# Convolution branch and gates as a Strassen stage of their own ahead of the attention, in a one-layer streaming encoder on one core

## The chip, the core and the metric

The kernel runs on one core of one Trainium2 chip. Its time is the device time of one execution in microseconds; the profile shows five engines that work side by side: PE (matrix multiply), DVE (vector), ACT (scalar), POOL (GpSimd) and SP, which here only issues DMAs. Before the change the median of three runs is 2145.94 us (2143.27 to 2147.6). Lower is better.

## The reference

One layer, 1024 prompt rows and 32 sample rows (T = 1056 columns in all), model width 1024. In short:

```python
h = rms_norm(x, norm1_g) * (1 + scale1) + shift1       # shift, scale, gate from silu(c) @ w_ada
q, k, v, xin, gb, gc, ga_br, gb_br = split(h @ w_in)   # eight sections of 1024 columns
o = diff_attention(norm(q), norm(k), v)                # 8 heads, chunk-causal for the prompt
y_a = sub_norm(o) @ w_attn_out
y_b = (gb * short_conv(gc * xin)) @ w_conv_out
m = sigmoid(ga_br) * y_a + sigmoid(gb_br) * y_b
x = x + gate1 * (m @ w_out)
x = x + gate2 * ((silu(g) * up) @ w_down)              # g, up = split(norm2(x) @ w_gate_up)
```

## The kernel before, in words

Everything is float32. A matrix operand is split in two parts (`split`: ACT makes the high part, DVE or POOL subtracts it for the low part), and each product is three matmuls: high by high, high by low, low by high. The activations lie transposed, 128 channels by 1056 columns, in eight tiles; a weight piece is 1024 rows by 128 columns.

The program has these stages, in order of time.

- **Head.** Loads x, computes norm1 and the modulation (matmuls of `w_ada`), and writes the split operand `hh`, `hl` (`modulate`). The first attention matmul ends it.
- **Attention and convolution, interleaved.** Per head, eight prompt tiles of 128 rows and one sample tile. A tile is a projection (`proj`, L485 to L487, 24 matmuls of 384 columns) and then five steps in `attend`: transposes of q and k (L372), scores (L397, L398), transposes of the probabilities (L434), probabilities by values (L448), transpose of the result (L461). Between two steps, ACT, DVE and POOL work on the tile: the epilogue, the split of q and k (L359 to L365), the softmax (L403 to L422), the copy of the transposed probabilities (L443), the last norm (L450 to L457). The convolution branch (`conv`, L526 to L528) is 72 units of 24 matmuls of 352 columns, for the sections xin, gc and gb. Its weight pieces are split with POOL for the low part.
- **Gates.** The sections ga and gb, 48 units of 24 matmuls of 352 columns (L687 to L689), each piece followed by one `ada_step`: one of 32 later modulation chunks, 16 DVE instructions (`adacc`) and, one step later, two transposes on PE (`pad`).
- **Attention output projection, convolution output projection, w_out, gate and up, down.** The gate-and-up stage already uses Strassen's product (`strassen`, L1013): of a pair of weight pieces and four quarters of the columns it makes seven products of 12 matmuls of 264 columns in place of eight.

The order of PE's instructions is the order in which the program is written. In the attention stage a small planner in the kernel writes it: it holds a clock that counts an assumed cost of each PE step and an assumed wait behind it (8.0 us behind a projection, 4.0 behind the q and k transposes, 4.5 + 6.5 L/1024 behind the scores, 1.2 and 4.0 behind the next two). A tile's next step is placed as soon as its assumed wait is over, otherwise a projection or a convolution unit is placed. At most MAXRUN = 4 tiles are under way, and behind a head's last projection no new one starts for RELOAD = 9.0 us, because the next head's weights take the place of the old. The order on the other engines is set by the compiler's scheduler.

PSUM in the attention stage has two buffers `mm` for projections, two `tr` for all transposes and small products (steps 1, 3, 4 and 5, one after the other in rotation; step 3 takes two when it has over four blocks), and two `S` for scores. The head's weights `qh`, `ql` have one buffer, and are staged in two: the third of the three sections is loaded when the first has been split.

```python
MAXRUN, RESERVE, RELOAD = 4, 3, 9.0
...
if pnext is not None and len(running) < MAXRUN and clock >= hold and (
        cnext is None or pdone * (9 * KT - RESERVE) <= cdone * 9 * H):
    unit_now, kind = pnext, 0
elif cnext is not None and (pnext is not None or True):
    unit_now, kind = cnext, 1
```

Of the kernel before, what the change touches and what calls it, by code (L numbers as in the profile page):

```python
# [14 lines left out]
P = 128  # L15
# [23 lines left out]
def hybrid_layer(tc, x_prompt, x_sample, cache_k, cache_v, state_conv, c_prompt, c_sample,  # L39
# [19 lines left out]
    m1_d = dram.tile([KT, P, T], F32, name="m1_d")  # L59
# [6 lines left out]
    hTp = sb("hT", side="right")  # L66
# [18 lines left out]
    def wload(src, hi, lo, lo_eng=None, v=None):  # L85
        if v is None:
            v = stage()[:, :1024].rearrange("p (a b) -> p a b", a=src.shape[1])
        sp.dma_start(v, src)
        split(v, hi, lo, lo_eng)

    def wpiece(src, lo_eng=None):
        hi = W.tile([P, KT, P], F32R, tag="wh", name="wh", bufs=2)
        lo = W.tile([P, KT, P], F32R, tag="wl", name="wl", bufs=2)
        wload(src, hi, lo, lo_eng)
        return hi, lo
# [23 lines left out]
    hh = hTp.tile([P, KT, T], F32R, name="hh")  # L119
    hl = hTp.tile([P, KT, T], F32R, name="hl")  # L120
    hS = hTp.tile([P, KT, P], F32R, name="hS")
    dve.memset(f(hS), 0.0)

    qW = sb("qW")

    def load_qkv(h):
        hi = qW.tile([P, 3, KT, P], F32R, tag="qh", name="qh")
        lo = qW.tile([P, 3, KT, P], F32R, tag="ql", name="ql")
        for j in range(3):
            v = qW.tile([P, KT, P], F32, tag="qst", name="qst", bufs=2)  # L130
            wload(win_v[:, :, j * D + h * P:j * D + (h + 1) * P], hi[:, j], lo[:, j], None, v)
        return hi, lo


    X0 = sb("X0")
    PS0 = ps("PS0")
    vec = const.tile([P, P], F32, name="vec")
    sc = const.tile([P, 16], F32, name="sc")
    pv = PS0.tile([P, 512], F32, tag="b", name="pv", bufs=2)
# [9 lines left out]
    def rows_to_vec():  # L149
        pv = PS0.tile([P, 512], F32, tag="b", name="pv", bufs=2)  # L150
        pe.transpose(pv[:, :P], rows, ident)
        dve.tensor_copy(vec, pv[:, :P])
# [6 lines left out]
    def attention_constants():  # L159
        lams = X0.tile([P, 4, HD], F32, name="lams")  # L160
# [6 lines left out]
        lprod = X0.tile([P, 2, HD], F32, name="lprod")  # L167
        dve.tensor_mul(lprod, lams[:, 0:2, :], lams[:, 2:4, :])
        lsum = X0.tile([P, 2], F32, name="lsum")
# [14 lines left out]
    xts = {}  # L184

    def x_norm(i):

        src, n = token_tile(i)
        xt = X0.tile([P, D], F32, tag="xt", name="xt", bufs=5)
        sp.dma_start(xt[:n], src)  # L190
        junk = X0.tile([P, D], F32, tag="junk", name="junk", bufs=1)
# [4 lines left out]
        xts[i] = xt, n  # L196

    def x_transpose(tiles, kts):
        q0 = tiles[0] * P
        w = sum(xts[i][1] for i in tiles)  # L200
        for kt in kts:
            pt = PS0.tile([P, 512], F32, tag="x", name="pt", bufs=4)
# [1025 lines left out]
```

## Time and profile before

| what | value |
|---|---|
| median of the runs | 2145.94 us (2143.27 to 2147.6) |
| the profiled execution's own time | 2149.89 us |
| its span, first to last instruction | 2148.1 us |
| PE, DVE, ACT, POOL busy, share of the span | 96%, 57%, 36%, 18% |
| granted PE clock, mean | 0.987 |
| head | 0 to 64.1 us |
| attention and convolution | 64.1 to 906.6 us |
| gates | 906.6 to 1097.0 us |
| both output projections | 1097.0 to 1287 us |
| w_out, gate and up, down | 1287 to 2148 us |

A row of the grouped view gives line, engine, operation, output and input tiles, shapes and count, then the busy time and the mean of one in ns. Matmuls overlap, so the mean of one (about 325 ns for 352 columns) is longer than the step from one to the next; the step is read from a stage's length and its count. A row of the view by windows gives a stretch, its length, the busy time and instruction count of PE, PE's weight loads, DVE, ACT and POOL, then the granted PE clock, the DMA share and GB/s.

### The profile page before, as it was taken

What the parts mean: (1) busy time and instruction counts of PE and PEld (TensorE: products, weight loads), DVE (VectorE), ACT (ScalarE), POOL (GpSimd) and SP (SyncE); (2) the same over time, 40 slices, a digit from 0 to 9 for tenths busy, and PEclk for the clock granted to TensorE, in tenths of its full rate; (3) what the DMA queues carried; (4) which work ended last, traced back from release to release, by engine and by line L of the source; (5) the groups of instructions that cost most, each with busy time, mean ns of one, the idle gap of its engine ahead of it and who ended that gap; (6) DMA issues with size and microseconds to landing.
All of it is one profiled execution on the core that took longest, in us unless ns stands there. A gap on an engine that the chain in (4) does not pass through costs nothing. (4 is left out here: it accounts for less than half of the span.)

```text
span 2148.1 us, 36100 instructions
## 1 busy us (share of the span) xinstructions
PE 2060.6 (96%) x13955; PEld 2014.5 (94%) x13955; DVE 1215.7 (57%) x2775; ACT 770.8 (36%) x1875; POOL 384.8 (18%) x644
## 2 busy tenths in 40 slices
PE   7899999999999999999999999879999999989999
PEld 5799998989899989899999999879999999989998
DVE  5665656575747465556567884576555556432322
ACT  5344445454545444423221112363332332321210
POOL 2333323333333332200000000002112112100000
PEclk9999999999999999999999999999999999999999
DMA  9312122121212110255567634223222222551321
GB/s 261 86 45 60 43 61 60 46 58 46 71 34 72 34 50 23 58 162 180 170 210 224 205 113 142 66 70 108 83 80 84 76 80 74 174 156 53 109 69 57
DMA packets 286195, 206.93 MB, mean 96 GB/s; under 512 B 12976, under 2 KB 269768, under 8 KB 286024
## 3 DMA queue, kind: packets, MB, share of 16 engines
q1 hardware_dynamic: 286024, 204.63, 31.5%
q8 instruction: 110, 1.80, 0.4%
q14 instruction: 61, 0.50, 0.1%
HBM read 153.74 MB, written 50.84 MB: 95 GB/s over the span
## 5 line engine op out<-in xcount | busy, mean ns | idle before, releaser
L82 ACT CAST ws<-st 128x512 fp32r<-128x512 f32 (+1 forms) x280 | 170.1, 614 | 451.4 <-PE u L1013 107.1
L83 DVE TENSOR_TENSOR ws<-st,ws 128x512 fp32r<-128x512 f32 (+1 forms) x258 | 179.4, 701 | 248.6 <-ACT ws L82 246.8
L1013 PE MATMUL u<-T,ws 128*128 128x264 f32 x1848 | 237.6, 285 | 7.8 <-ACT T L82 6.5
L1013 PEld LDWEIGHTS u<-T,ws 128*128 128x128 f32 x1848 | 230.2, 189 | 8.4 <-ACT T L82 6.7
L526 PE MATMUL mm<-hh,wh 128*128 128x352 f32 x576 | 199.2, 346 | 0.0
L528 PE MATMUL mm<-hh,wl 128*128 128x352 f32 x576 | 188.6, 327 | 0.0
L527 PE MATMUL mm<-hl,wh 128*128 128x352 f32 x576 | 188.3, 327 | 0.0
L485 PE MATMUL mm<-qh,hh 128*128 128x384 f32 x512 | 184.3, 360 | 3.0 <-ACT hh L82 2.9
L487 PE MATMUL mm<-qh,hl 128*128 128x384 f32 x512 | 174.5, 341 | 0.0
L486 PE MATMUL mm<-ql,hh 128*128 128x384 f32 x512 | 173.9, 340 | 0.0
L1013 PE MATMUL u<-B,ws 128*128 128x264 f32 x1320 | 170.9, 283 | 0.0
L1013 PEld LDWEIGHTS u<-B,ws 128*128 128x128 f32 x1320 | 164.2, 188 | 0.2 <-ACT p L1017 0.2
L1130 PE MATMUL u<-ka,ws 128*128 128x352 f32 x480 | 157.6, 328 | 4.6 <-ACT ka L82 2.9
L1131 PE MATMUL u<-ka,ws 128*128 128x352 f32 x480 | 156.5, 326 | 2.6 <-DVE ka L83 2.6
L1132 PE MATMUL u<-ka,ws 128*128 128x352 f32 x480 | 156.1, 325 | 0.0
L414 ACT ACTIVATE p<-S,nmx,rs 128x128 f32<-128x128 f32 (+5 forms) x144 | 113.5, 790 | 117.5 <-DVE nmx L410 76.5
L242 DVE SCALAR_TENSOR_TENSOR adacc<-adw,sc,adacc 128x128 f32<-128x128 f32 x448 | 130.6, 349 | 0.6
L687 PE MATMUL u<-hh,ws 128*128 128x352 f32 x384 | 125.9, 328 | 0.0
L689 PE MATMUL u<-hh,ws 128*128 128x352 f32 x384 | 124.9, 325 | 0.0
L688 PE MATMUL u<-hl,ws 128*128 128x352 f32 x384 | 124.2, 323 | 0.0
L687 PE MATMUL u<-oh,ws 128*128 128x352 f32 (+1 forms) x384 | 123.2, 321 | 0.0
L689 PE MATMUL u<-oh,ws 128*128 128x352 f32 (+1 forms) x384 | 121.0, 315 | 0.0
(263 smaller groups left out, 4767.5 us busy)
## 6 DMA issues: line engine op xcount, KB each, us to landing
st<-in_w_gate_up_dram SPq DMA_DIRECT2D x44, 512.0 KB, 4.1
adw<-in_w_ada_dram SPq DMA_DIRECT2D x43, 512.0 KB, 4.3
st<-in_w_in_dram SPq DMA_DIRECT2D x40, 512.0 KB, 4.3
qst<-in_w_in_dram SPq DMA_DIRECT2D x24, 512.0 KB, 4.7
sa<-a_d SPq DMA_DIRECT2D x22, 528.0 KB, 3.7
a_d<-xa SPq DMA_DIRECT2D x84, 132.0 KB, 1.8
st<-in_w_down_dram SPq DMA_DIRECT2D x16, 512.0 KB, 4.3
z_d<-z SPq DMA_DIRECT2D x24, 176.0 KB, 2.7
```

Of the source, the lines that this page charges most:

```text
L82: act.copy(hi, src)
L83: (lo_eng or dve).tensor_sub(lo, src, f(hi))
L485: pe.matmul(pj[:, 0:384], a, qh[:, :, kt, :], start=kt == 0, stop=False)
L486: pe.matmul(pj[:, 0:384], a, ql[:, :, kt, :], start=False, stop=False)
L487: pe.matmul(pj[:, 0:384], b, qh[:, :, kt, :], start=False, stop=kt == KT - 1)
L526: pe.matmul(pt[:, :gw], wh[:, kt, :], hh[:, kt, g0:g0 + gw], start=kt == 0, stop=False)
L527: pe.matmul(pt[:, :gw], wh[:, kt, :], hl[:, kt, g0:g0 + gw], start=False, stop=False)
L528: pe.matmul(pt[:, :gw], wl[:, kt, :], hh[:, kt, g0:g0 + gw], start=False, stop=kt == KT - 1)
L687: pe.matmul(pt[:, :gw], wh, ah[:, kt, g0:g0 + gw], start=kt == 0, stop=False)
L689: pe.matmul(pt[:, :gw], wl, ah[:, kt, g0:g0 + gw], start=False, stop=kt == KT - 1)
L1013: pe.matmul(q[dst], l, t[:, r, j, :], start=first and j == n == 0, stop=j == 3 and n == 2, skip_group_check=not first)
L1130: pe.matmul(pt[:, :gw], wh, ah, start=kt == 0, stop=False)
```

## The change

Five of the eight sections (xin, gc, gb, ga, gb_br) are computed by `strassen` in a dense stage ahead of the attention. `h_operands` makes the seven operands of the activations for each of the two column groups right behind the modulation, and the modulated x is also written to memory (`h_d`). The convolution is done on pairs of channel tiles, between the Strassen products of gc and gb. The two gate sections follow, with two `ada_step` for each pair. Then `h_d` is loaded back, tile by tile, and split as the operand of q, k and v (`hA`), in the slots of the Strassen operands.

The attention follows without the convolution units. The planner has MAXRUN = 5 and RELOAD = 7.0, and when a head's weights hold it up it places nothing. When no projection is left, units of the convolution's output projection (`wco_units`) fill its last part; the rest of them and the attention's output projection follow, with the operand tiles in other slots. In the head, x is loaded first and the `w_ada` chunks behind it; the modulation matmul has weights and activations exchanged (`ada_matmul`).

The diff, cut to its core:

```diff
-    hh = hTp.tile([P, KT, T], F32R, name="hh")
-    hl = hTp.tile([P, KT, T], F32R, name="hl")
...
+    def h_operands(j, g):
+        def parts(o, src):
+            t = Top[o, g]
+            split(src, t[:, 0, j, :], t[:, 1, j, :])
+        b11, b12 = (xnT[:, j, q * QW:(q + 1) * QW] for q in (g, g + 2))
+        b21, b22 = (xnT[:, j + 4, q * QW:(q + 1) * QW] for q in (g, g + 2))
+        t1, t2, t3 = (X0.tile([P, QW], F32, tag=f"t{i}", name="ht", bufs=1) for i in (1, 2, 1))
+        parts("B11", b11)
+        dve.tensor_sub(t1, b12, b11)
+        dve.tensor_sub(t2, b22, t1)
+        parts("T2", t2)
+        parts("T1", t1)
...
+    for j in range(4):
+        for i in range(4):
+            ada_matmul()
...
+        modulate(j)
+        modulate(j + 4)
+        h_operands(j, 0)
+        if j:
+            h_operands(j - 1, 1)
+    for n in range(KT):
+        sp.dma_start(h_d[n], xnT[:, n, :])
+    h_operands(3, 1)
...
+    for p in range(0, KT, 2):
+        xin = pair_tile()
...
+            conv_in(wstrassen(win_pair(3, p)), p, (0, 1), xin)
+        w = wstrassen(win_pair(5, p))
...
+        conv_gate(w, p, u, xin)
+        w = wstrassen(win_pair(4, p))
...
+        conv_out(w, p, z)
...
+    for sec, dst in ((6, ga_d), (7, gb_d)):
+        for p in range(0, KT, 2):
+            w = wstrassen(win_pair(sec, p))
...
+            strassen(w, (0, 1), dest, epi)
+            ada_step()
+            ada_step()
+    while ada_open:
+        ada_open.pop(0)()
...
+    for t in range(8):
+        v = kt_stage(hv[:, :, t * P:(t + 1) * P])
+        hA.append(op_slot(t, [P, 2, KT, P], F32R, "hA"))
+        split(v, hA[t][:, 0], hA[t][:, 1])
...
-    MAXRUN, RESERVE, RELOAD = 4, 3, 9.0
+    MAXRUN, RELOAD = 5, 7.0
...
-            if pnext is not None and len(running) < MAXRUN and clock >= hold and (
-                    cnext is None or pdone * (9 * KT - RESERVE) <= cdone * 9 * H):
-                unit_now, kind = pnext, 0
-            elif cnext is not None and (pnext is not None or True):
+            if pnext is not None:
+                if len(running) < MAXRUN and clock >= hold:
+                    unit_now, kind = pnext, 0
+            elif running and cnext is not None:
                 unit_now, kind = cnext, 1
...
-    for sec, dst in ((6, ga_d), (7, gb_d)):
-        for n in range(KT):
-            w = wpiece(win_v[:, :, (sec * KT + n) * P:(sec * KT + n + 1) * P])
...
-                unit(pt, w, hh, hl, g0, gw)
-                act.activation(sg[:, g0:g0 + gw], pt[:, :gw], AF.Sigmoid)
-            sp.dma_start(dst[n], sg)
...
-            ada_step()
```

Two places show how the order moves. The first is PE at the end of a middle head, from the sample tile's last projection matmuls (`hS`) on. Before, convolution matmuls (L526 to L528) follow, with steps of the tiles under way among them:

```order
2576 L511 MATMUL mm<-qh,hS 128x384
2577 L512 MATMUL mm<-ql,hS 128x384
2578 L526 MATMUL mm<-hh,wh 128x352
2579 L527 MATMUL mm<-hl,wh 128x352
2580 L528 MATMUL mm<-hh,wl 128x352
2581 L526 MATMUL mm<-hh,wh 128x352
2582 L527 MATMUL mm<-hl,wh 128x352
2583 L528 MATMUL mm<-hh,wl 128x352
2584 L461 MATMUL tr<-ident,on 128x128
```

After, the last result transpose (L697), the q and k transposes of the eighth tile (L608), the probability transposes of the sixth (L670, six of them), its values product (L684) and the scores of the eighth (L633, L634) stand one behind the other, and the next head's projection (L721) is next:

```order
1492 L748 MATMUL mm<-ql,hS 128x384
1493 L697 MATMUL tr<-ident,on 128x128
1494 L608 MATMUL tr<-ident,qd 128x128 x2
1495 L608 MATMUL tr<-ident,kd 128x128 x2
1496 L670 MATMUL tr<-ident,p 128x128 x6
1497 L684 MATMUL tr<-V,aT 128x128 x6
1498 L633 MATMUL S<-K,QH 128x512
1499 L634 MATMUL S<-K,QL 128x512
...
1505 L634 MATMUL S<-K,QL 128x512
1506 L721 MATMUL mm<-qh,hA 128x384
```

What moved: the convolution matmuls that stood between the steps are gone, and steps that use the two `tr` buffers follow each other directly.

The second is DVE in the gates stage. Before, each weight piece (two `ws`) has one `adacc` group of 16:

```order
1252 L251 TENSOR_REDUCE adred<-pad 128x2
1253 L239 TENSOR_SCALAR adacc<-adw,sc 128x128
1254 L252 TENSOR_SCALAR mod<-adred,vec 128x2
1255 L242 SCALAR_TENSOR_TENSOR adacc<-adw,sc,adacc 128x128
1256 L239 TENSOR_SCALAR adacc<-adw,sc 128x128
1257 L242 SCALAR_TENSOR_TENSOR adacc<-adw,sc,adacc 128x128 x12
1258 L83 TENSOR_TENSOR ws<-st,ws 128x512
1259 L242 SCALAR_TENSOR_TENSOR adacc<-adw,sc,adacc 128x128
1260 L83 TENSOR_TENSOR ol<-st,oh 128x1056
1261 L83 TENSOR_TENSOR ws<-st,ws 128x512
```

After, for each pair of pieces, two such groups stand among the weight sums and splits (L142 to L152, L84) and the sums of the Strassen products (L183, L186, L192):

```order
660 L183 TENSOR_TENSOR u_5481<-u,p_5451 128x264
661 L332 SCALAR_TENSOR_TENSOR adacc<-adw,sc,adacc 128x128 x5
662 L186 TENSOR_TENSOR w<-u,u_5466 128x264
663 L332 SCALAR_TENSOR_TENSOR adacc<-adw,sc,adacc 128x128 x4
664 L186 TENSOR_TENSOR w<-u,u_5481 128x264
665 L332 SCALAR_TENSOR_TENSOR adacc<-adw,sc,adacc 128x128 x4
666 L84 TENSOR_TENSOR ws<-st,ws 128x512
667 L332 SCALAR_TENSOR_TENSOR adacc<-adw,sc,adacc 128x128
668 L142 TENSOR_TENSOR st<-st 128x512
669 L84 TENSOR_TENSOR ws<-st,ws 128x512
670 L144 TENSOR_TENSOR st<-st 128x512
671 L147 TENSOR_TENSOR st<-st 128x512
```

What moved: the modulation chunks stand in a stage whose products also need DVE for every sum, and on PE the last chunk's two transposes stand ahead of the first attention matmul.

629 lines of the change are left out of this document (325 added, 304 removed).

## The prediction

> **What bounds the kernel now.** I read the page's busy times first, then the view by windows, cut at the stages, then PE's waits and the rows behind them.
>
> ```profile
> PE 2060.6 (96%) x13955; PEld 2014.5 (94%) x13955; DVE 1215.7 (57%) x2775; ACT 770.8 (36%) x1875; POOL 384.8 (18%) x644
> ```
>
> ```profile
> 0.00:64.10 64.10, 43.86 (x347) 31.73 (x347) 39.75 (x97) 33.40 (x73) 20.41 (x31) 1.00 0.92 257
> 64.10:906.60 842.50, 807.78 (x5096) 780.51 (x5096) 504.63 (x1194) 395.56 (x1179) 277.38 (x522) 0.98 0.17 50
> 906.60:1097.00 190.40, 190.40 (x1185) 189.81 (x1184) 106.78 (x334) 50.85 (x93) 0.00 (x0) 0.99 0.56 169
> 1429.60:1867.00 437.40, 437.37 (x3596) 437.37 (x3597) 250.09 (x460) 142.07 (x284) 79.92 (x86) 1.00 0.29 86
> ```
>
> PE is the bound: it is never idle in the gates (third row) and in gate-and-up (fourth), and in the attention stage it is busy 807.8 of 842.5 us. Those 35 us are mostly one kind of wait:
>
> ```profile
> PE tr L461 <- DVE on L457: 21.0, 13, 2.2
> L457 DVE SCALAR_TENSOR_TENSOR on<-o,rn,gsub x72: 339/352/2440, 99.9 to 906.0; 128x128 f32<-128x128 f32 x64, 32x128 f32<-32x128 f32 x8
> L83 POOL TENSOR_TENSOR wl<-st,wh 128x1024 fp32r<-128x1024 f32 x24 | 58.1, 2420 | 34.1 <-ACT wh L82 34.0
> ```
>
> The last norm of a tile on DVE takes 0.35 us, but up to 2.44 where one of the 24 convolution weight splits on POOL (2.42 us) runs, and PE then waits about 2 us. What such a wait does to PE's speed shows in the time line behind one of them:
>
> ```profile
> 766.99 0.30 PE L461 MATMUL tr<-ident,on 128*128 128x128 f32 x1 [2.03 <-DVE on L457]
> ...
> 768.30 0.50 PE L526 MATMUL mm<-hh,wh 128*128 128x352 f32 x1
> 768.60 0.50 PE L527 MATMUL mm<-hl,wh 128*128 128x352 f32 x1
> ...
> 771.65 0.32 PE L526 MATMUL mm<-hh,wh 128*128 128x352 f32 x1
> 771.80 0.32 PE L527 MATMUL mm<-hl,wh 128*128 128x352 f32 x1
> ```
>
> Matmuls of 352 columns start 0.30 us apart for some 3.4 us after the wait, and 0.16 apart later: PE runs at half its clock for that time and loses about 1.7 us more.
>
> **The matmuls that go.** The chain of waits has gate-and-up as one piece:
>
> ```profile
> 1429.63 433.59 PE u L1013 x3563
> ```
>
> So a Strassen matmul of 264 columns costs 433.59 / 3563 = 0.1217 us. One of 352 columns costs 190.40 / 1184 = 0.161 us (the gates row). The change turns 5 sections x 8 pieces x 3 groups x 24 = 2880 matmuls of 352 into 5 x 4 pairs x 7 x 2 x 12 = 3360 of 264: 463.7 becomes 408.9 us. That is the gain, 55 us: in the convolution 278.2 (1728 x 0.161) becomes 245.3 (2016 x 0.1217), in the gates 185.5 becomes 163.6. All the rest is about what the convolution had been covering.
>
> **Gates: DVE takes the bound.** Durations from the Strassen stage and from the gates of before:
>
> ```profile
> L83 DVE TENSOR_TENSOR ws<-st,ws 128x512 fp32r<-128x512 f32 x126 | 91.6, 728 | 91.9 <-ACT ws L82 90.4
> L988 DVE TENSOR_TENSOR st<-st 128x512 f32<-128x512 f32 x21 | 15.0, 712 | 0.7
> L1020 DVE TENSOR_TENSOR u<-u,p 128x264 f32<-128x264 f32 x42 | 17.9, 427 | 4.7 <-PE u L1013 4.7
> L242 DVE SCALAR_TENSOR_TENSOR adacc<-adw,sc,adacc 128x128 f32<-128x128 f32 x224 | 63.7, 349 | 0.1
> L239 DVE TENSOR_SCALAR adacc<-adw,sc 128x128 f32<-128x128 f32 x32 | 8.8, 282 | 0.6 <-PE u L689 0.6
> L251 DVE TENSOR_REDUCE adred<-pad 128x2 f32<-128x256 f32 x14 | 5.9, 425 | 11.1 <-PE pad L249 11.1
> ```
>
> A gate pair asks DVE for 6 low parts, 4 weight sums and 10 product sums: 6 x 0.73 + 4 x 0.71 + 10 x 0.43 = 11.5 us. Two modulation chunks add 2 x (14 x 0.349 + 2 x 0.282 + 0.425 + some 0.3) = 12.4. So DVE needs 23.9 us for a pair whose matmuls take 168 x 0.1217 + 0.4 = 20.9. Only two chunks can run ahead (two `adacc` buffers), so 7 of 8 pairs are paced by DVE: 20.9 + 7 x 23.9 = 188. The last chunk starts only when its buffer is free, behind the last pair, and its transposes stand ahead of the first attention matmul, so its 5.5 us of DVE lie in the open; the first pair, which has no chunk beside it, gives part of that back. I take 190, no gain against 190.4. Bounds are 167 (all of DVE hidden, 8 x 20.9) and 197 (the last chunk and some of the split of `hA`, which is DVE work too, on top).
>
> **Head and convolution.** The head of before moved 257 GB/s (first row of the windows). x now comes first, 4.3 MB or 17 us; norm, transposes and four chunks of `w_ada` bring the first operands to about 35. Their rows:
>
> ```profile
> 25.59 3.82 PE L205 MATMUL pt<-ident,xt 128*128 128x128 f32 x32
> 29.34 1.91 PE L221 MATMUL pa<-adw,sc 128*2 128x128 f32 x16
> ```
>
> From there DVE sets the pace: in its order 61 instructions of 264 columns, 10 of 512 and some 24 small ones stand ahead of the low part that the first product waits for. At 0.38 (0.728 scaled to 264 columns; 0.43 with PSUM) that is 23 + 7 + 5.5 = 36 us. First matmul near 72 (bounds 64 and 78), 8 later than before. The convolution then needs 245 us of PE. A pair of its channel tiles takes 3 x 20.4 = 61 us of PE and, on DVE, 3 x 11.5 and some 12 for the taps, which PE's matmuls hide; were they not hidden, each pair would cost what DVE is over 61. I add 5 us for a start at half clock and for second-group operands that are made late: 250 (247 to 260). The stores of `h_d` and its loads (4.3 MB each way) run on DMA queues that were 0.17 to 0.56 busy in these stages; on SP the stores stand ahead of the loads for the second product, which has 20 us until it needs them. I count them at nothing.
>
> [...]
>
> **Attention without filler.** The stage of before, less 278 for the convolution, is 564.5 us: 530 of PE busy and 35 of waiting. What waits now is read from measured latencies along the new order. Three rules give nearly all of it. First, the weights:
>
> ```profile
> L512 PE MATMUL mm<-ql,hS x3: 334/334/334, 576.2 to 576.9; 128*128 128x384 f32 x3
> L82 ACT CAST qh<-qst x3: 1046/1047/1052, 577.1 to 583.9; 128x1024 fp32r<-128x1024 f32 x3
> L83 DVE TENSOR_TENSOR ql<-qst,qh x3: 1217/1224/1226, 578.2 to 585.0; 128x1024 fp32r<-128x1024 f32 x3
> L485 PE MATMUL mm<-qh,hh x1: 338/338/338, 589.7 to 589.7; 128*128 128x384 f32 x1
> ```
>
> The last sample matmul ends at 577.3, the third low part at 586.2: a reload takes 9.0 us, and before, the next projection came at 12.4, behind convolution work. RELOAD is now 7.0, and the order has only some 4.5 us of matmuls there. Second, the two `tr` buffers:
>
> ```profile
> 508.45 0.38 PE L372 MATMUL tr<-ident,kd 128*128 128x128 f32 x2
> ...
> 509.23 0.47 ACT L359 ACTIVATE K<-tr,gq 128x256 fp32r<-128x256 f32 x1
> ...
> 509.59 0.37 ACT L361 CAST QH<-tr 128x256 fp32r<-128x256 f32 x1
> ...
> 510.78 0.42 DVE L365 TENSOR_TENSOR QL<-tr,QH 128x256 fp32r<-128x256 f32 x1
> ```
>
> The q and k transposes end at 508.83 and their buffer is read until 511.20: 2.4 us, of which the instructions themselves are 0.47 + 0.37 + 0.42 = 1.3. A step that needs the same buffer two uses later now follows at once, where convolution matmuls stood between. Third, the copy behind the probability transposes:
>
> ```profile
> L443 DVE COPY aT<-tr 128x512 f32<-128x512 f32 x8 | 5.4, 675 | 0.6 <-PE tr L434 0.6
> ```
>
> ```profile
> 772.12 0.40 PE L397 MATMUL S<-K,QH 128*128 128x512 f32 x1
> 772.36 0.40 PE L398 MATMUL S<-K,QL 128*128 128x512 f32 x1
> ```
>
> The copy takes about 0.9 us with its start, and the values product can now follow the transposes directly. The two score rows give the step of a score matmul, 0.24 us.
>
> At the end of a head (second piece of the order) this gives: L697 and the eighth tile's transposes take 0.5 us, four of the six L670 0.4, the fifth waits 2.4 - 0.4 = 2.0 for the buffer, it and the sixth take 0.2, L684 waits 0.9 and takes 1.3, the scores take 8 x 0.24 = 1.9, and L721 finds 7.2 of the 9.0 us gone and waits 1.8. The waits are 4.7 us for a head.
>
> Inside a head the same rule meets, by the order, the fourth tile's transposes (1.3), the fifth's (2.0), the sample cache's (0.9) and one or two later ones (0.3 to 2): another 5 to 6. So about 10 us a head, 80 in all; 8 at the shortest latencies of the trace, 13 to 17 if the denser stage slows the chains (DVE was 60% busy, and the same work without the convolution's now falls in three quarters of the time). With four waits of about 2 us a head, of which roughly every other one of before was followed by the half clock at 1.7 us, the clock costs 25, where in the 530 of before it cost about 17 (a granted clock of 0.98 over 842.5). With 5 of those 8 on top I take 85: 530 + 85 = 615. Bounds: 565, for idle of 35 as before, and 670, for 17 a head.
>
> [...]
>
> **The sum.** 72 + 250 + 190 + 615 = 1127 up to the point where before stood at 1097.0; the output projections and all that follows keep their matmuls (four units of the convolution's projection, 15 us, move up into the attention's last part; I count them where they were). 2148.1 + 30 = 2178; the profiled execution lies 1.8 above its span and 4 above the median. On the median: 2145.9 + 30 = **2176 us**.
>
> **The rivals.** *A: the attention fills itself.* With POOL's long splits gone the chains come down to their own instructions, 1.3 to 1.8 us for the buffer, so idle is 45 to 60 in place of 85; and the scheduler hides part of the modulation chunks, gates 178. Then 70 + 248 + 178 + 585 = 1081: 16 us faster, 2130; at best, with every bound at its low end, 2100. For it speaks that nearly half of the 2.4 us was waiting in a queue; against it that the reload and the buffer rotation are fixed by buffer counts. It decides when the attention's idle time stays below 55 us, with the other terms as taken. *B: the half clock settles in.* If each of some 40 waits of 2 us or more costs a window of 3.4 us, and the in-order queues of DVE and ACT add a microsecond to each chain, each head waits 17 us, 140 in all, and the attention takes 670: 72 + 250 + 190 + 670 = 1182, 85 slower, 2231. Against it: only about half of such waits did so before. *C: it cancels.* Idle of 51 to 59 us with the other terms as taken makes the sum 1093 to 1101, within 4 us of before: 2146.
>
> **How the numbers follow.** Forecast (slower by 10 to 65 us) 0.50, A 0.27, B 0.15, C 0.08. A difference under 0.2%, 4 us, cannot be told from none here. The range reaches into A and B until a tenth is left out on each side: 2118 to 2224; the forecast's own is 2156 to 2211. Faster 0.27, same 0.08, slower 0.65.
>
> **What would show it.** In the changed profile: PE busy in 0.12 us steps through the convolution with hardly a gap; a gates stage near 190 us with DVE close to full; in the attention PE waits at L721 for `ql` at each head (1 to 4 us), at L670 and L684 for the q and k split or the copy, and more stretches at half clock. I am wrong if the gates are near 167, or if PE's idle time in the attention is under 55 us.

## The result, and the profile after

The changed kernel takes 2253.74 us (2249.89 to 2259.23, four runs) against 2146.55 us (2143.27 to 2147.6, four runs): a ratio of 1.0504, 95% interval 1.0476 to 1.0532. It is 107 us slower, 78 us above the forecast and 30 above the range. The page of the changed kernel has these two lines for the engines' busy time and the clock in 40 slices:

```profile
PE 2081.6 (92%) x14419; PEld 2018.5 (89%) x14419; DVE 1377.8 (61%) x3128; ACT 841.6 (37%) x2033; POOL 392.9 (17%) x688
```

```profile
PEclk7699999998999999999899999999999999999999
```

PE's busy time did not fall, though 55 us of matmuls went; it rose by 21, and the span rose by 109. The view by windows, cut at the stages (head, convolution, gates, attention, the attention's last part with four units of the convolution's projection), has the columns of the prediction (length, then busy time and count of PE, weight loads, DVE, ACT and POOL, then granted clock, DMA share and GB/s):

```profile
0.00:82.90 82.90, 66.77 (x330) 64.54 (x331) 40.17 (x113) 39.66 (x80) 9.58 (x24) 0.67 0.64 208
82.90:342.40 259.50, 250.27 (x2017) 249.34 (x2018) 202.20 (x408) 73.07 (x142) 67.81 (x98) 0.97 0.26 77
342.40:519.20 176.80, 167.36 (x1379) 166.56 (x1376) 155.12 (x423) 66.89 (x140) 13.07 (x11) 0.98 0.50 154
519.20:1184.60 665.40, 558.84 (x3267) 508.51 (x3268) 400.31 (x999) 356.94 (x1097) 207.37 (x450) 0.93 0.17 50
1184.60:1215.90 31.30, 29.96 (x199) 27.34 (x198) 20.00 (x47) 15.97 (x46) 6.49 (x15) 1.00 0.27 83
```

| stage | before | predicted | measured |
|---|---|---|---|
| head | 64.1 | 72 | 82.9 |
| convolution | 278.2 | 250 | 259.5 |
| gates | 190.4 | 190 | 176.8 |
| attention without filler | 564.5 | 615 | 681.2 |
| sum | 1097 | 1127 | 1200 |

The attention's figure is 665.4 + 31.3, less 15.5 for the 96 filler matmuls in it. The two Strassen stages together brought 32 us (18.7 and 13.6), where the forecast had 28, all of it in the convolution. The head lost 18.8 and the attention 117; what follows takes 6 us more. PE's waits by what it waited for (us in total, times, longest):

```profile
PE tr L670 <- ACT ot L699: 18.5, 15, 4.3
PE tr L670 <- ACT aT L679: 12.7, 8, 3.8
PE tr L697 <- DVE QL L601: 12.1, 9, 2.1
...
PE mm L721 <- ACT qh L83: 7.2, 3, 2.5
PE S L634 <- DVE QL L601: 6.7, 7, 2.3
PE tr L697 <- DVE on L693: 6.7, 5, 1.7
```

Where before one kind of wait made most of the idle time, now no single one has a fifth of the 108 us. The longest one, in the time line of PE and ACT:

```profile
840.46 0.27 PE L697 MATMUL tr<-ident,on 128*128 128x128 f32 x1
...
840.48 1.04 ACT L83 CAST qh<-st 128x1024 fp32r<-128x1024 f32 x1 [2.08 <-PE mm L747]
...
841.43 1.09 ACT L650 ACTIVATE p<-S,nmx,rs 128x896 f32<-128x896 f32 x1
...
842.51 1.03 ACT L83 CAST qh<-st 128x1024 fp32r<-128x1024 f32 x1
...
844.07 1.10 ACT L650 ACTIVATE p<-S,nmx,rs 128x896 f32<-128x896 f32 x1
...
845.15 0.26 ACT L699 COPY ot<-tr 128x128 f32<-128x128 f32 x1
...
845.46 0.90 PE L670 MATMUL tr<-ident,p 128*128 128x128 f32 x3 [4.30 <-ACT ot L699]
```

The result of a tile is transposed by 840.73, and its copy takes ACT 0.26 us. But the copy stands in ACT's queue behind two weight casts, two exponentials and a short copy, which ACT works off with hardly a gap (3.36 us busy of the 3.41 from 840.92 on), and PE needs that `tr` buffer back: 4.30 us.

What such a wait does to the clock shows in windows of 3.41 us, cut where the granted clock changes (the clock is the column behind POOL's):

```profile
837.50:840.92 3.42, 3.42 (x22) 3.20 (x20) 1.53 (x3) 1.22 (x4) 1.06 (x3) 1.00 0.00 0
840.92:844.33 3.41, 0.24 (x3) 0.01 (x1) 3.21 (x7) 3.36 (x6) 0.00 (x0) 1.00 0.00 0
844.33:847.74 3.41, 1.30 (x5) 0.90 (x6) 3.28 (x7) 3.41 (x11) 0.30 (x2) 0.50 0.80 216
847.74:851.16 3.42, 2.15 (x9) 1.75 (x9) 2.56 (x6) 0.71 (x1) 1.79 (x4) 0.50 0.42 122
851.16:854.57 3.41, 3.41 (x13) 2.93 (x12) 0.33 (x3) 0.77 (x3) 0.76 (x2) 0.50 0.54 154
854.57:857.99 3.42, 3.42 (x21) 2.77 (x19) 3.00 (x7) 1.92 (x5) 0.00 (x0) 1.00 0.00 0
```

A window in which PE works 0.24 us is followed by one at half clock; that one has 1.30 us of work, and the next is at half clock too, and so on, until a window full of work (the fifth row) ends it: in the last row the clock is full.

### The profile page after: what moved, and what is told of

Its sections match the earlier page's. It is cut to its first block, busy times and chain, and to the rows that moved or that the text cites. A ratio compares the mean times of both kernels' runs of the same rounds, so it can differ in the third digit from the quotient of the medians.

```text
span 2257.4 us, 37877 instructions
## 1 busy us (share of the span) xinstructions
PE 2081.6 (92%) x14419; PEld 2018.5 (89%) x14419; DVE 1377.8 (61%) x3128; ACT 841.6 (37%) x2033; POOL 392.9 (17%) x688
## 5 line engine op out<-in xcount | busy, mean ns | idle before, releaser
L83 ACT CAST ws<-st 128x512 fp32r<-128x512 f32 (+1 forms) x388 | 234.9, 615 | 576.3 <-PE u L176 177.9
L176 PE MATMUL u<-op,ws 128*128 128x264 f32 x3168 | 393.5, 284 | 7.8 <-ACT op L83 6.5
L176 PEld LDWEIGHTS u<-op,ws 128*128 128x128 f32 x3168 | 388.7, 189 | 8.4 <-ACT op L83 6.7
L84 DVE TENSOR_TENSOR ws<-st,ws 128x512 fp32r<-128x512 f32 (+1 forms) x346 | 242.3, 707 | 201.5 <-ACT ws L83 199.0
L721 PE MATMUL mm<-qh,hA 128*128 128x384 f32 x512 | 188.6, 368 | 8.4 <-ACT qh L83 7.2
L722 PE MATMUL mm<-ql,hA 128*128 128x384 f32 x512 | 175.6, 343 | 2.1 <-DVE ql L84 2.1
L723 PE MATMUL mm<-qh,hA 128*128 128x384 f32 x512 | 175.3, 342 | 0.0
L84 POOL TENSOR_TENSOR ws<-st,ws 128x512 fp32r<-128x512 f32 x42 | 55.1, 1311 | 491.7 <-ACT ws L83 434.3
L721 PEld LDWEIGHTS mm<-qh,hA 128*128 128x128 f32 x512 | 99.0, 193 | 12.0 <-ACT qh L83 8.1
L580 POOL TENSOR_TENSOR rs<-rs,mhalf 128x2 f32<-128x2 f32 x144 | 101.1, 719 | 5.9
L722 PEld LDWEIGHTS mm<-ql,hA 128*128 128x128 f32 x512 | 98.9, 193 | 3.4 <-DVE ql L84 3.1
L1202 PEld LDWEIGHTS u<-ka,ws 128*128 128x128 f32 x480 | 91.6, 191 | 8.4 <-ACT ka L83 5.6
L684 PE MATMUL tr<-V,aT 128*128 128x128 f32 (+2 forms) x608 | 92.3, 301 | 7.1 <-DVE QL L601 3.1
```

The lines of the kernel that those rows point to most:

```text
L83: act.copy(hi, src)
L84: (lo_eng or dve).tensor_sub(lo, src, f(hi))
L176: pe.matmul(q[dst], l, t[:, r, j, :], start=first and j == n == 0, stop=j == 3 and n == 2, skip_group_check=not first)
L580: pool.tensor_tensor(out=rs[:n, c:c + 2], in0=rs[:n, c:c + 2], in1=mhalf[:n, 0:2], op=ALU.pow)
L721: pe.matmul(pj[:, 0:384], a, qh[:, :, kt, :], start=kt == 0, stop=False)
L722: pe.matmul(pj[:, 0:384], a, ql[:, :, kt, :], start=False, stop=False)
```

## The experiments

Theory after the result: without filler, PE meets the latency of each step's answer, and it pays for that in idle time and in half clock. The rivals: one buffer ring is short (`tr`; a ring is a set of buffers used in rotation), one queue is too full (ACT's or DVE's), the planner's distances are too short, the weight reload blocks the end of each head, or the new stages and layout themselves are slower. Totals are medians of two runs, to be held against 2254 us (its own runs differ by 9 us, so differences under some 5 us say nothing). "Net" is the attention's length less 0.161 us for each filler matmul in it, 681 us in the changed kernel and 564 before.

**Filler back in.** Dummy units stand where the convolution's units stood, placed by the rule of before.

```diff
-    MAXRUN, RELOAD = 5, 7.0
+    def fill_units():
+        for i in range(72):
+            def run(i=i):
+                pt = mm_tile()
+                x = hA[(i + 1) % 8][:, 0].rearrange("p k c -> p (k c)")[:, :GW]
+                for kt in range(KT):
+                    for n in range(3):
+                        pe.matmul(pt[:, :GW], hA[i % 8][:, n % 2, kt, :], x, start=kt == n == 0,
+                                  stop=kt == KT - 1 and n == 2)
+                    yield 3 * 0.161
+            yield run()
...
+    MAXRUN, RESERVE, RELOAD = 4, 3, 9.0
...
```

> 72 units of 24 matmuls of 352 columns on the resident operand, whose sums nobody reads, stand in the attention where the kernel before had its convolution, by that kernel's rule of order (MAXRUN 4, RELOAD 9.0); the convolution's projection units all follow behind the attention. The units are 278 us of matmuls at 0.161 us. If the lost filler is the cause, the attention takes 278 + 530 + 35 to 45 of idle time = 843 to 855 us, so 565 to 577 without the units, and the total is 2395 to 2420. If the dense stage, the new layout or the crowded engines were the cause, the attention takes 278 + 640 to 681 and the total is 2490 to 2530.

Measured: 2387.79 us, below what was expected. The attention takes 822.0 us:

```profile
516.50:1338.50 822.00, 804.39 (x5096) 772.82 (x5096) 423.93 (x1037) 378.59 (x1137) 217.77 (x464) 0.99 0.14 40
```

PE is idle 17.6 us, and the net is 544: 137 less than in the changed kernel and 20 less than before. So the layout, the operands and the engines' load are not what costs; the missing independent matmuls are. The planner's old rule does not explain it either: with that rule and no filler a head takes 96.5 us (below). Much of the 20 us below the kernel before is the wait for the last norm on DVE, 21.0 us there and 4.9 here. With POOL's 24 convolution splits gone that norm takes 0.35 us at most in the changed kernel (up to 2.44 before).

**The buffer ring.** The values product and the result's transpose use `mm`.

```diff
-        po = tr_tile()
+        po = mm_tile()
...
-        pt = tr_tile()
+        pt = mm_tile()
         pe.transpose(pt[:, :n], on[:n], ident[:n, :n])
```

> The values product and the transposes of a tile's result take their PSUM buffer from the ring mm, which only the projections use otherwise, so the ring tr serves the q and k transposes and the probability transposes alone. Ring theory (a step waits because the buffer two uses back is still being read; the two waits of L670 and L697 are 66 of the 109 us that PE idles in the attention): at least 40 us of that idle time go, and some 15 us of half clock with it; total 2195 to 2215. Queue theory (the answers of ACT and DVE are late whatever buffer is used): the waits move to the projections and to L684, the idle time stays above 95 us; total 2240 to 2260.

Measured: 2253.7 us, idle 110.4 us. The waits moved:

```profile
PE tr L670 <- ACT aT L679: 27.9, 12, 6.0
PE mm L721 <- ACT sq L575: 13.5, 10, 2.4
```

The ring theory, which was also the frame of my forecast, fell. At L670 the waits on `ot` are gone, and others, as long, came up there and at the projections. The run moves load from one pair of buffers to another and adds none, so whether there are too few buffers in all is not tested.

**One queue for another.**

```diff
-        act.copy(ot[:, :n], pt[:, :n])
+        dve.tensor_copy(ot[:, :n], pt[:, :n])
```

> The copy of a tile's result out of PSUM (L699, 0.28 us) is made by DVE in place of ACT. If the buffer is held long because ACT's queue has long exponentials in front of that copy, the 15 waits of L670 on it (18.5 us) go and the total falls to 2225 to 2240. If DVE's queue, 60% busy in this stage, is as late, as many waits stand there with DVE as the releaser and the total stays within 8 us of 2254.

Measured: 2270.71 us, 17 more than the changed kernel, which neither side expected; idle 124.2 us. Waits for `ot` fell from 18.5 to 7.9 us at L670, and a wait that was hardly there (0.5 us) took their place, behind DVE's longer queue:

```profile
PE tr L670 <- DVE QL L601: 22.9, 6, 6.2
```

**The reverse.** The second copy of the probabilities goes from DVE to ACT.

```diff
-                (act.copy if b0 == 0 else dve.tensor_copy)(aT[:w, i0:i1, :n], pt[:w, i0:i1, :n])
+                act.copy(aT[:w, i0:i1, :n], pt[:w, i0:i1, :n])
```

> The copy of the fifth to eighth transposed probability block (L679, 32 times in the attention, 0.4 to 0.7 us) is made by ACT in place of DVE, the reverse of the move of 20 us from ACT to DVE that cost 17 us. If DVE is the queue that counts, 8 to 17 us less, 2237 to 2246. If every queue counts alike, or the two copies side by side were worth more, the total stays the same or rises: 2250 to 2270.

Measured: 2240.47 us, 13 less, as if DVE were the queue that counts; but in the traces the attention accounts for 7 us (689.8 in place of 696.8), and the head, which this edit does not touch, for 3.4.

**Less in DVE's queue.**

```diff
-        dve.scalar_tensor_tensor(out=kd[HD:P], in0=ksrc[HD:P], scalar=gq[HD:P], in1=f(kd[HD:P]),
-                                 op0=ALU.mult, op1=ALU.subtract)
```

> Left out: the subtraction that makes the low part of the keys on partitions 64 to 127 (L598, 0.49 us on DVE, 63 times in the attention, 31 us), so that the keys are the high part alone. It stands ahead of the query's low part in DVE's queue. If the waits are made by the load of the in-order queues, the idle time falls by 20 us or more and the total by 20 to 40 us, to 2214 to 2234. If they are made by distances in the order or by buffers, it falls by what the one chain is shorter where PE waits for QL (22 us in 19 waits of about 1.2 us): under 12 us, total 2242 to 2250.

Measured: 2236.42 us, 17 less, with idle time of 94.5 us, 13 less: between the two cases. So I took the larger load of the row maximum out as well:

```diff
-                dve.tensor_reduce(out=nmx[:n, m:m + 1], in_=sv[m][:n], axis=AX.X, op=ALU.max, negate=True)
-                dve.tensor_mul(nmx[:n, m:m + 1], nmx[:n, m:m + 1], rs[:n, m:m + 1])
...
-            act.activation(p[:n, :L], sv[m][:n], AF.Exp, bias=nmx[:n, m:m + 1], ...
+            act.activation(p[:n, :L], sv[m][:n], AF.Exp, bias=zero1[:n], ...
```

> Left out: the row maximum of the scores and its product with the norm (L639, L640, L645, L646, some 105 us of DVE in the attention); the exponentials take a bias of zero, and the scores are a quarter of what they should be so that they stay finite. Queue theory (what is in DVE's queue sets when a tile's answers come; 31 us less of DVE gave 16 us, 20 us moved onto DVE cost 17): 50 to 85 us less, total 2170 to 2205, idle time of PE in the attention below 70 us. If only the length of one chain or the order counts, the two score buffers are read some 1.4 us less and a tile's answer comes as much earlier, but PE still waits at L670 and L697 for ACT's copies: 10 to 30 us less, total 2225 to 2245.

Measured: 2245.24 us (2241.71 and 2248.77), just beyond the second case. DVE has 322 us of work in the attention where the changed kernel had 420 (400.31 + 20.00), the time from the last score matmul to the blended probabilities is 3.5 us in place of 5.6 (medians), and PE is still idle 101.7 us. The largest wait grew, from 18.5 us:

```profile
PE tr L668 <- ACT ot L697: 27.9, 19, 3.7
```

So the load of DVE's queue is not the cause either; a hundred microseconds less of it gave some 8. Whether the same work counts where there is filler:

> The kernel before, with the same left out as in the changed kernel without row maximum (and the scores a quarter). If convolution work hides what DVE does in the attention, the total changes by less than 6 us, 2140 to 2150. If DVE's time counts there too, it falls as far as in the changed kernel, 50 us or more.

Measured: 2152.89 us for the kernel before with the same left out, 1.0025 (1.0013 to 1.0036) of its time, though DVE has 390 us of work in the attention in place of 505. With filler the maximum was hidden altogether.

**More distance.** MAXRUN 7, longer assumed waits, one to three more buffers for twelve small tiles.

```diff
-    MAXRUN, RELOAD = 5, 7.0
+    MAXRUN, RELOAD = 7, 7.0
...
-        yield 0.43, 4.0
+        yield 0.43, 6.0
```

> The planner may keep 7 tiles in flight in place of 5, counts on longer answers (10, 6, 6 + 6.5 L/1024, 2.5 and 5 us in place of 8, 4, 4.5 + 6.5 L/1024, 1.2 and 4), and the small tiles of the attention have a buffer or more to spare. If PE idles because the order places a step before its answer is there, though other matmuls would be ready, the idle time of 108 us falls below 60 and the total to 2180 to 2205. If the answers only come later still, because ACT and DVE work through the same queue whatever the order, or the eight PSUM buffers hold the tiles back, the idle time stays above 90 us and the total above 2235.

Measured: 2237.16 us, idle 100.3 us, net 666: the second case. From the end of its projection to its result a tile takes 50 us in place of 37 (medians), and the wait now sits at the scores' two buffers, which took 4.9 us in the changed kernel:

```profile
PE S L633 <- ACT p L650: 33.2, 15, 5.7
```

An order in which the exponentials come later:

```diff
+        yield 4 * max(0.213, L / 2400), 1.0 + 2.6 * L / 1024
         pr = []
...
-        yield 4 * max(0.213, L / 2400), 4.5 + 6.5 * L / 1024
+        yield 0.0, 3.5 + 3.9 * L / 1024
```

> The order alone changes: the two exponentials and the blend of a tile are issued as a step of their own, 1 + 2.6 L/1024 us behind the scores by the planner's clock, so that short copies issued meanwhile can stand ahead of them. If exponentials that wait for DVE's maximum block ACT's queue, the waits of L670 and L697 fall by 20 us or more, total 2210 to 2235. If ACT's order is not what holds the copies, within 8 us of 2250, either way.

Measured: 2243.95 us, idle 104.5 us: 10 us less, inside the second case (2242 to 2258). The exponentials in front of the copies are not the one cause.

**No reload.**

```diff
-        if h + 1 < H:
-            qkv_w[0] = load_qkv(h + 1)
```

> Left out: the loading and splitting of the q, k and v weights of heads 1 to 7; all heads use those of head 0. That takes 21 casts of 1.05 us from ACT and 21 subtractions of 1.22 us from DVE, in the second part of each head, and the waits at L721. PE's longest waits (4.3 us at L670 for a copy of 0.27 us that stood behind two casts and two exponentials in ACT's queue) lie there. If those casts make the long waits, the idle time falls by 25 to 50 us and the half clock with it, total 2195 to 2225. If only the waits at L721 and L722 for the weights themselves count (9.3 us), total 2240 to 2250.

Measured: 2228.04 us, nearer the first case and the largest effect of a single edit: 26 us, 24 of them in the attention. Idle fell by only 13 us, to 94.6, all of it within 15 us behind the heads' ends (43 us of idle time there, then 30). The time at half clock fell from 90 us to 63, which gives the other 11. So 24 us of the attention's loss hang on the reload, most of them not at its own line (L721 and L722, some 9 us of waits). The long waits are not the casts' alone: without them the longest wait just behind a head's end is still 3.59 us, at the same line.

**How much filler.** The edit is shown against the run with 72 units.

```diff
-        for i in range(72):
+        for i in range(24):
...
-                    cnext is None or pdone * (9 * KT - RESERVE) <= cdone * 9 * H):
+                    cnext is None or pdone * (24 - RESERVE) <= cdone * 9 * H):
```

> As the run with 72 units of filler without a reader, with 24 units (93 us of matmuls at 0.161 us), spread evenly. With 72 units the attention took 822 us, 544 without the units. If what filler covers is in proportion to its amount, a third of the cover brings the attention to 681 - 46 = 635 us without the units, total 2290 to 2310. If a little of it in every gap does nearly all, it is 560 to 590 without the units, total 2235 to 2260. If it needs all 72, it stays over 660 and the total over 2330.

Measured: 2358.79 us, net 698: the third case by its numbers; but the rule had not spread the units. It used some 8 in each of the first three heads and none behind. The two parts by windows:

```profile
518.20:826.20 308.00, 293.12 (x1827) 277.77 (x1828) 157.28 (x383) 140.01 (x416) 78.64 (x172) 0.99 0.15 42
826.20:1308.80 482.60, 384.50 (x2120) 344.29 (x2118) 261.67 (x656) 235.44 (x725) 136.07 (x292) 0.88 0.15 42
```

The first three heads, with filler, take 308.0 - 92.7 = 215 us, 72 a head. The other five, with four tiles in flight and nothing to fill, take 96.5 a head. A thin spread needed another rule, shown against the changed kernel:

```diff
-    MAXRUN, RESERVE, RELOAD = 4, 3, 9.0
+    MAXRUN, RELOAD = 5, 7.0
...
+            if pnext is not None and len(running) < MAXRUN and clock >= hold:
+                unit_now, kind = pnext, 0
+            elif cnext is not None and cdone * 9 < (pdone + 1) * 4:
+                unit_now, kind = cnext, 1
```

> 32 units of filler without a reader (124 us of matmuls at 0.161 us), placed only where the changed kernel's planner itself finds nothing to issue, at most 4 ahead of each head's share; MAXRUN 5 and RELOAD 7.0 as in the changed kernel; the convolution's projection units all follow behind. If half the filler in the right places does nearly all, the attention without the units takes 560 to 600 us (681 in the changed kernel, 544 with 72 units) and the total is 2257 to 2297. If cover goes by the amount, 32 of 72 units give 61 of the 137 us back: 620 us, total 2317. If the waits lie where the planner sees none, it stays above 645 us, total above 2342.

Measured: 2303.24 us, four units a head:

```profile
518.70:1249.90 731.20, 666.02 (x4137) 624.57 (x4138) 424.22 (x1039) 370.99 (x1139) 209.16 (x464) 0.99 0.16 45
```

The net is 731.2 - 123.6 = 608, between the first and the second case: 53% of what 72 units gave back, for 44% of them. Idle is still 65 us, but the granted clock is back at 0.99. A microsecond of filler covers 0.59 us here and 0.49 with 72 units: less than its own price, so 124 us of filler without a reader make the whole kernel 49.5 us slower.

**The head.** The modulation matmul in the form of before, beside nothing else.

```diff
-            pe.matmul(pa[:, 0:2], v[:, kt, :], sc[:, kt:kt + 9:8], start=kt == 0, stop=kt == KT - 1)
+            pe.matmul(pa[0:2, :P], sc[:, kt:kt + 9:8], v[:, kt, :], start=kt == 0, stop=kt == KT - 1)
+        act.copy(row, pa[0:2, :P])
...
+            pe.transpose(pb[:, 0:2], row, ident[0:2, 0:2])
```

> The modulation matmul of the head has its old form (activations as weights, 128 columns of w_ada moving, a copy and a transpose behind it); all else is the changed kernel. If the exchanged form with its 3.3 us a chunk sets the head's length, the head falls from 82.9 us to 62 to 70 and the total to 2232 to 2242. If the DVE work of the operands or the transfers set it (DVE's order asks for some 36 us behind the first operands), the head stays at 78 to 83 and the total within 6 us of 2254.

Measured: 2239.32 us, 14 less, 1.0417 (1.0387 to 1.0448) of before; the head ends at 69.2. Changed kernel first (the rows of L318 alone: length, PE, weight loads, granted clock, DMA share, GB/s), then this one:

```profile
30.02:31.93 1.91, 1.91 (x17) 1.91 (x18) 1.00 0.03 9
31.93:43.09 11.16, 11.16 (x55) 11.16 (x54) 0.50 0.49 141
43.09:60.00 16.91, 16.91 (x81) 16.91 (x80) 0.50 0.55 157
```

```profile
0.00:69.20 69.20, 47.63 (x347) 36.40 (x347) 39.34 (x105) 41.96 (x93) 10.68 (x25) 0.94 0.75 241
```

A chunk is 16 records. The exchanged form runs at 1.91 / 17 = 0.11 us a record, 1.8 us a chunk, for two microseconds; then the clock falls to half, and it is 16.91 / 81 = 0.21 a record, 3.3 a chunk, to the head's end.

**Head and gates.**

```diff
             strassen(w, (0, 1), dest, epi)
-            ada_step()
-            ada_step()
+            if (sec, p) != (7, KT - 2):
+                ada_step()
+                ada_step()
+            while ada_open and (sec, p) == (7, KT - 4):
+                ada_open.pop(0)()
```

> The head with the old form of the modulation matmul, and the gates without chunks of the modulation behind the last pair (the last open chunks are closed behind the pair before; the two left over go to the output projections). If the 8.3 us that PE waits for the last chunk's sums at the end of the gates are all that the chunks cost there, the stage from the first gate product to the first attention matmul falls by 7 to 9 us and the total is 2230 to 2234. If DVE paced the pairs too, the gates fall by more than 12; if the split of the attention's operand ends last anyway, by less than 3 and the total stays at 2237 to 2241.

Measured: 2240.66 us, and from the first convolution product to the first attention matmul 433.2 us against 436.0 with the head alone: the third case by its number, but not for its reason. The second row here is the first attention matmul:

```profile
476.84 0.30 PE L346 MATMUL pad<-ident,adacc 128*128 128x128 f32 x1 [5.13 <-DVE adacc L339]
501.15 0.34 PE L732 MATMUL mm<-qh,hA 128*128 128x384 f32 x1
```

The first attention matmul now follows the last gate product without a wait, so the split of the attention's operand does not end last. The wait for the chunks' sums moved: PE now waits 6.0 us for them one pair earlier, where the edit closes the open chunks, in place of 8.8 at the end and 1.2 more at the first attention matmul.

**The small gains together.** The edits of three runs above: the head, MAXRUN 7 with its waits and buffers, and the second copy on ACT.

> Three edits together: the head's modulation matmul in its old form (-14 alone), 7 tiles in flight with longer assumed answers and spare small buffers (-17 alone), and the second copy of the probabilities on ACT (-13 alone). If they act on different waits, 2254 - 14 - 17 - 13 = 2210; if the last two shift the same waits, 2218 to 2226.

Measured: 2219.81 us, 1.0333 (1.0279 to 1.0387) of before: the second case, and the fastest version here that has the new stages and computes the whole. None beats the kernel before.

## Why the prediction was wrong, step by step

The sign was right and the mechanism in kind: the convolution had been filler, and without it PE waits more and runs longer at half clock. The sum was 73 us short (1127 against 1200): 66 in the attention, 11 in the head and 9.5 in the convolution, less 13 in the gates. The step that failed most is the attention's price, and the others follow.

**The attention's price: 50 in place of 117.** The sum had 530 + 85, with 670 as its upper bound. The 85 were 80 of idle time and 5 for the clock. Measured idle is 108 us, and the time at half clock 90 us where before had 27. Taking from each stretch at half clock half of PE's busy time in it, and the idle time from the gaps between matmul records:

| us | before | changed | 72 units | 32 units |
|---|---|---|---|---|
| idle | 35 | 108 | 18 | 65 |
| lost to half clock | 13 | 37 | 7 | 10 |
| the rest, without filler | 516 | 536 | 520 | 532 |
| net | 564 | 681 | 544 | 608 |
| pauses between matmul records (a count, not us) | 25 | 109 | 32 | 96 |

So of the 117 us 73 are idle time, 24 the clock, and 20 lie in the rest. Against the forecast the idle time was mis-sized by 28 us (108 for 80), the clock by 19 (24 more than before, for 5), and the rest by 20, which I had held fixed. In the two traces the clock did not follow single waits but the idle time of a window of 3.41 us in all. Before, each of the 6 windows that the clock fell behind held one pause (1.88 to 2.29 us of it in the window); in the changed kernel, with no filler between the waits, 10 of 15 held two or three, and in 5 of them no pause alone was half a window (the longest 1.29 to 1.65 us, together 1.80 to 2.47). Once at half, the clock came back only behind a window with at most 0.33 us idle, so those 15 falls made 25 windows at half clock (before, 6 made 7; in each, one more reached in from the stage ahead). The rest has a likely cause, argued only: a matmul behind which PE pauses is counted with its whole length (0.27 us in the row at 840.46), in a dense row with its step, and there are 84 more pauses. The four columns agree: more pauses, a larger rest. The sum also took the waits of before out whole, and with them the 21.0 us for the last norm on DVE; no run shows by itself that those waits go with POOL's splits. In the changed kernel all 72 of these norms take 0.34 to 0.35 us, and PE still waits 6.7 us for them.

**The waits' kind: half right.** I forecast waits at L670 and L684 on the `tr` ring, and at L721 for the weights (1 to 4 us a head). L670 holds 40 of the 108 us, but L697, which I did not name, holds 26 and L684 only 7. The hold of a buffer by the q and k split is there (12.1 us at L697 in the list above), yet I took it for the cause. The ring experiment falsified that: with the `tr` ring relieved the idle time stayed (110). L721 and L722, which I priced at 1.8 a head, are some 9 us in all, while the reload as a whole costs 24.

What the experiments show is that filler takes the loss away (137 us for 72 units, 73 for 32), and that no one buffer, queue or distance does: eight edits gave between +17 and -26. Each takes its own wait away, and PE then stops at the next answer that is not there. That reads as a schedule with too little independent work behind every step; which share belongs to which engine's order is not settled. Replaying the planner's own arithmetic gives 53 us in which its clock jumps because it has nothing to place. That number could be had from the code, but it is half of the idle time and less than the 80 that I took: the planner's assumed waits are fixed numbers and know nothing of the engines' queues.

**The head: 72 in place of 82.9.** I took 1.91 us a chunk from before's row. In the changed kernel the operands of that matmul are exchanged, and I gave that no price. At the price measured, 16 chunks cost 53 us from 30.0 on. The experiment gives 13.7 us of the head back (82.9 to 69.2). DVE's pace, which I had let end the head, did not end last: PE goes through L318 without a gap up to 82.9. With the old form the head comes near my 72; no run shows whether DVE's pace sets it then.

**Convolution: 259.5, inside the bounds** (247 to 260). PE is idle for 9 us of it, 8 of them in its first 20 us, and the half clock of the head lasts 10 us into it; I had added 5 for both.

**Gates: 190 in place of 176.8.** I let DVE's 23.9 us a pair set the pace. One window of 22 us in the middle (the second number is PE's busy time, the fourth DVE's), ten instructions of the last chunk, and the end of the stage:

```profile
409.00:431.00 22.00, 22.00 (x184) 22.00 (x184) 21.17 (x62) 7.65 (x17) 1.29 (x1) 1.00 0.52 162
```

```profile
513.79 2.71 DVE L332 SCALAR_TENSOR_TENSOR adacc<-adw,sc,adacc 128x128 f32<-128x128 f32 x10
516.39 0.45 PE L339 MATMUL pad<-ident,adacc 128*128 128x128 f32 x1 [7.55 <-DVE adacc L332]
```

The durations of a middle pair's rows on DVE add up to 24.0 us, as I had them. But the rows overlap: a chunk's instructions are 0.34 us long and start 0.26 apart (ten of them take 2.71 us). So DVE is busy for 20.0 us of the 20.8 that a pair takes, does its two chunks in that time, and PE never waits for it inside a pair. The row that I quoted had part of this: 63.7 us busy for 224 instructions is 0.28 each, not the 0.349 that I multiplied. What is left is the last chunk, which I had put in the open: PE waits 7.55 us for it, and 1.9 more up to the first attention matmul. The stage is my lower bound of 167 plus that tail.

**The rivals.** Idle time of 108 us rules out A (below 55) and C (51 to 59). The result lies beyond B (2231), whose attention of 670 us comes nearest to 681. But it has 108 us of idle time where B had 140 in all, and the clock and the rest make the difference; the head, which no rival had, adds 11.

Two smaller things. A's best case, with every bound at its low end, adds up to 64 + 247 + 167 + 565 = 1043 and so to 2092, not 2100. And both signs that I named for being wrong, gates near 167 and idle time under 55, look for a faster kernel. The gates came half way there (176.8), the idle time did not come near, and the forecast was too low all the same.

## What to carry to other kernels

Work that can be made cheaper by moving it out may be worth more where it is: price it by what it covers, and get that price first by leaving it out or by putting matmuls without a reader in its place, which takes one run and settles what eight edits to buffers, queues and order could not. Where filler is scarce, try it where the planner's own clock would jump; 44% of the filler there gave 53% of the cover and nearly all of the clock (0.99 granted, 0.93 without filler). An exchange of a matmul's operands needs a price of its own (here 3.3 us a chunk in place of 1.91). And where an engine's rows overlap, its pace is read from its busy time, not from durations added up.

## What the runs showed of the hardware

In the traces of the kernel before and of the changed kernel the granted clock changes at whole steps of 3.413 us: in the changed kernel it is 1.00 from 837.50 to 844.33 us, two steps, and 0.50 from there to 854.57, three. The attention stages (first projection to last result) of the two traces hold 449 whole windows of that length, 246 before and 203 after. The table sorts them by the clock granted in the window and by the share of it in which PE has no matmul, and has how many of them were followed by a window at half clock:

| idle share of the window | window at full clock | window at half clock |
|---|---|---|
| below 10% | 0 of 326 | 0 of 23 |
| 10 to 20% | 0 of 18 | 2 of 2 |
| 20 to 40% | 0 of 38 | 5 of 5 |
| 40 to 50% | 0 of 9 | none |
| 50 to 60% | 5 of 8 | none |
| 60% and more | 16 of 16 | 4 of 4 |

So in these two stages the clock fell behind 21 windows, each idle for 1.80 to 3.17 us in one piece or in several, and behind none that was idle for less. At half clock it came back behind the 23 windows that were idle for 0.33 us at most, and behind none of the 11 that were idle for 0.57 us or more. A wait of the same length cost the half clock once and nothing another time: of two waits of 2.03 us in the kernel before, the one at 764.95 lay in one window and the next, from 768.00 on, was at 0.50; the one at 459.79 lay in two windows, 1.01 us in one and 1.02 in the other, and the clock stayed at 1.00. Of the 11 waits of 1.7 us or more there, the clock fell behind 6, and the other five all lay across the end of a window.

The matmuls with two moving columns in the head did not hold the clock. From 36 to 79 us of the changed kernel PE has no gap, by its records (43.00 us busy of 43.00), and the granted clock is 0.50. With 128 moving columns (and two columns of weights) in the same place, in the run with the head as before, PE is busy for 16.96 us of the 17.00 from 28 to 45 and for 18.36 of the 24.20 from 45 to 69.2, and the granted clock is 0.94 and 0.97. So a PE that is busy throughout by its records was not enough for the full clock here.
